# ScalarE places running sums into PSUM before the products: a diffusion step on one core

## The chip, the cores and the metric

The kernel runs on one core of one Trainium2 chip. A core has a matrix engine (TensorE, PE in the profile), which multiplies tiles of 128 by 128 with tiles of 128 by 512 and adds the products up in PSUM (8 banks of 128 by 512 f32), a vector engine (VectorE, DVE), a scalar engine (ScalarE, ACT), GpSimd (POOL) and SyncE (SP), which here issues the DMAs. Each engine runs its own instructions in the order in which the program emits them, and waits on semaphores for what other engines and DMAs deliver. The metric is the time of one execution on the device, in microseconds.

## The reference, cut to what matters

One layer of a diffusion backbone, for 128 context tokens and 128 latent tokens:

```
h   = RMSNorm(x) * (1 + scale1) + shift1          # scale, shift, gate: SiLU(cond) @ w_ada + b_ada
p   = h @ w_in                                    # 2048 x 8704: q, k, v of two mixers, two gates
o_A = window attention(q_A, k_A, v_A);  o_B = neighbourhood attention(q_B, k_B, v_B)
m   = (sigmoid(gate_A) * (o_A @ w_br_a) + sigmoid(gate_B) * (o_B @ w_br_b)) @ w_out
x   = x + gate1 * m
h2  = RMSNorm(x) * (1 + scale2) + shift2
x   = x + gate2 * (relu(h2 @ w_up) ** 2 @ w_down)  # w_up 2048 x 8192, w_down 8192 x 2048
```

Both token groups use the same weights. Everything is f32, and the result must be near f32. The outputs are the new x of both groups and the new keys and values.

## The kernel before

**Products.** TensorE takes its operands rounded (`F32R`). Each f32 operand is therefore split in two, a rounded part (hi) and what the rounding left (lo), and a product is three matmuls: hi x hi, hi x lo, lo x hi. The weights come in 456 steps, `wsteps`. A step is one DMA of 512 KB (a tile of 128 by 1024: two slices of 128 rows, 512 columns), its preparation and, as a rule, 12 matmuls: 2 slices, 2 token groups, 3 products. The preparation (`prep`) is a ScalarE copy `wH<-raw` (hi, line 93) and a VectorE subtraction `wL<-raw,wH` (lo, line 241). For the steps of `LO_DMA` the lo part is made without VectorE: ScalarE writes minus hi (line 247), and a DMA of the GpSimd queue adds the raw weight to it (line 248).

**Order.** The program is written out step by step by `run`. At step i it emits the loads up to i + RUN[i] (each load is registered four steps ahead of its use), then the preparations up to i + LOOK[i], then the matmuls of step i, then whatever was hung on step i: `ex(i, ...)` first, then `at(i, ...)` in the order of registration. The tables (LOOK, RUN, DOTS and so on) are plain lists in the program. A position in the emitted order is a position in the queue of every engine: an instruction that waits holds up all that its engine has behind it.

**SBUF and PSUM.** All big tiles are taken from one pool of 48 buffers of 4 KB per partition (`G`). PSUM has two pools of four banks: `pacc` for running sums, `paux` for the rest. A unit of work is 512 output columns for both token groups and takes two banks of `pacc`, so two units fit at a time.

**First part (steps 0 to 71).** The nine units of q, k and v (`first_units`) go through their 16 slices in five chunks of 2, 2, 2, 4 and 6 slices (`CHUNKS`), because the normalised h appears slice by slice: `mod_pair` multiplies the condition with w_ada (64 small matmuls for each pair of slices, line 308), `make_h` scales (lines 354 and 356) and `split_h` splits (lines 93 and 97). A chunk has all nine units, each with 1, 1, 1, 2 or 3 steps. The last two units of a chunk stay in PSUM and open the next one; the others leave: after the first time ScalarE copies the sums to SBUF (`first_evac`), after later chunks VectorE adds them to the sums there (line 406, two instructions per unit). Chunk 4 is steps 27 to 44, in the order qB0, qB1, kB0, kB1, vB0, vB1, kvA, qA0, qA1; chunk 5 is steps 45 to 71.

**Middle (steps 72 to 215).** Gates, branch products, `w_out`, and the first two of the 16 column blocks of `w_up`. VectorE also forms the adaLN rows that do not come from `mod_pair`: `dot` (line 1339), 1024 elements at a time, hung on the steps of `DOTS1`, `DOTS` and `DOTS2`.

**Last part (steps 216 to 455).** For p = 0 to 7 the step list holds the next pair of blocks of `w_up` (`up_pair`, 16 steps) and then the four units of `w_down` over the pair p (`down_unit(p, n)`, n = 0 to 3, 4 steps each). In `up_pair`, 8 pairs of steps are worked either plainly (24 matmuls) or fast, by seven products in place of eight (21 matmuls, more VectorE and ScalarE work: lines 1184 to 1194); FAST lists the fast positions. The sum over p lies in SBUF, in `dsum[n]`: p = 0 is copied there by ScalarE; later ones are added by VectorE (line 1269, two instructions), or, for the units in `SUM_DMA`, copied by ScalarE to a tile that a DMA of the GpSimd queue adds (line 1273). After p = 6, `gate_sum` multiplies the sum with gate2 and adds it to x (lines 1250 and 1251, four VectorE instructions a unit); the products of p = 7 go through `resid` (lines 916 and 917) to the output. `gate_rows` (line 1352) is a TensorE transposition of the rows that the dots leave, hung on the first `down` step after the last dot.

The functions that the change touches:

Of the kernel before, what the change touches and what calls it, by code (L numbers as in the profile page):

```python
# [46 lines left out]
LOOK = "652422234122454433223333332123333453344534333554455544344534333543324554444555556665556644444333333333332222122312344544555434333333342344333334333323445566643344456656433344434444445455564546555553444554322466554554433333333434334533333333333654544332334455643444555653315536554523333334543233333332223323365455455443222212233432443334434642333334444544534434333333333325434222223333434444444434555642255242433444442233554442233242223342112224442233345544"  # L47
RUN = "300000000000010212223333322222222221111122244455544355434445554334554445555775654544345434444445665543321222222212444444444444442222222232223344444455544544444444555454454466677755566555554543365434343355445756644443566664333312222234552332223333334545332333333333322211133333332233311101234434433332332112444444442454322211333343334323233334544422742222212223445554422333233322222211222333333435767445344121210002232000233455555566567556433435335553333334"
CONST_AT = [67, 70]
XL_DMA = []  # L50
ADA_AT = [None, 4, 13, 16, 21, 36, 32]
XS_AT = {1: 13, 2: 18, 3: 29}
POST = {('kvA', 0): [67, 70, 75], ('qA', 0): [70, 73, 78], ('qA', 1): [72, 74, 80], ('kB', 0): [77, 86, 90], ('qB', 0): [82, 84, 93], ('kB', 1): [87, 92, 95], ('qB', 1): [90, 93, 96]}
JOBS = [[79, 80, 80, 87, 93], [81, 83, 88, 90, 93], [87, 87, 89, 90, 96], [93, 93, 96, 102, 105], [96, 97, 100, 105, 112], [102, 103, 107, 112, 123], [105, 107, 111, 118, 123], [112, 115, 118, 121, 123]]
SS_AT = [41, 57, 73, 75, 135, 139]
T_AT = [4, 4]
PREP_IN = [6, 4]
DOTS = [33, 39, 42, 45, 47, 48, 49, 50, 53, 55, 55, 55, 60, 65, 69, 70, 73, 75, 80, 84, 90, 91, 92, 93, 95, 100, 101, 103, 103, 104, 108, 110, 111, 112, 115, 118, 120, 122, 123, 124, 126, 127, 128, 129, 130, 132, 133, 134, 137, 138, 138, 143, 144, 145, 147, 150, 153, 157, 159, 160, 166, 167, 170, 172, 173, 174, 175, 176, 178, 178, 179, 183]
DOTS2 = [230, 232, 234, 235, 236, 237, 240, 243, 255, 263, 265, 269, 270, 288, 300, 300, 306, 328, 328, 331, 333, 334, 358, 360, 362, 364, 368, 368, 391, 391, 395, 399]
STAT_AT = [-1, 0, 10, 11]  # L60
T_PAIR = [[10, 8], [6, 8], [8, 10], [5, 7], [10, 13], [8, 9], [12, 11]]
P_PAIR = [[5, 2], [2, 4], [3, 5], [-1, 3], [5, 8], [3, 3], [7, 4]]
M_TE = (3,)
M_AT = [1, 3, 8]
FLIP = 1
P_UP = [2, 2]
T_UP = [7, 5]
COL = {"qA": 0, "kvA": 1024, "qB": 1536, "kB": 2560, "vB": 3584, "gA": 4608, "gB": 6656}
# [3 lines left out]
def tile_hybrid_step(ctx: ExitStack, tc: tile.TileContext, a):  # L72
# [209 lines left out]

    def mm3(acc, stat, st, first, last, order=(0, 1)):

        wh, wl = st["hl"]
        for k in range(2):
            kk = 2 * st["half"] + k
            for tb in order:
                sh, sl = stat(kk, tb)
                f, l = first and k == 0, last and k == 1  # L290
                pe.matmul(acc[tb], sh, wh[:, k, :], start=f, stop=False)  # L291
                pe.matmul(acc[tb], sh, wl[:, k, :], start=False, stop=False)  # L292
                pe.matmul(acc[tb], sl, wh[:, k, :], start=False, stop=l)  # L293

# [76 lines left out]

    open_acc = {}

# [4 lines left out]

    def start_steps(u, k0, nk, held, hold):


        box = {}

        def mm(st, kt):
            if kt == 0:
                box["acc"] = open_acc.pop(u) if held else [bank("acc", pacc) for _ in range(2)]
            acc = box["acc"]
            wh, wl = st["hl"]
            last = kt + 2 == nk
            for k in range(2):  # L390
                g, kg = divmod(k0 + kt + k, 4)
                for tb in range(2):
                    sh, sl = hH[g][:, kg, tb, :], hL[g][:, kg, tb, :]
                    pe.matmul(acc[tb], sh, wh[:, k, :], start=kt == 0 and k == 0 and not held, stop=False)  # L394
                    pe.matmul(acc[tb], sh, wl[:, k, :], start=False, stop=False)  # L395
                    pe.matmul(acc[tb], sl, wh[:, k, :], start=False, stop=last and k == 1 and not hold)  # L396
            if not last:
                return
            if hold:
                open_acc[u] = acc  # L400
                return
            if u not in units:
                first_evac(u, acc)
                return
            for tb in range(2):
                dve.tensor_tensor(units[u][:, tb, :], units[u][:, tb, :], acc[tb], op=OP.add)
# [117 lines left out]

    def unit(w, c0, ktiles, stat, evac, key, order="both"):

        box = {}
        n = len(ktiles)
        for j, k0 in enumerate(ktiles):
            def mm(st, j=j):  # L530
                if j == 0 and st["half"] == 0:
                    box["acc"] = [bank("acc", pacc) for _ in range(2)]
                mm3(box["acc"], stat(j), st, j == 0 and st["half"] == 0, j == n - 1 and st["half"] == 1)
                if j == n - 1 and st["half"] == 1:
                    evac(box["acc"])
            add_w(w, k0, c0, mm, key)
# [525 lines left out]

    def last_unit(w, c0, ktiles, stat, evac_s, key):

        box = {"hl": {}}
        n = 2 * len(ktiles)

        def mms(q, tb):
            wh, wl = box["hl"][q]
            for k in range(2):  # L1070
                sh, sl = stat(q // 2)(2 * (q % 2) + k, tb)
                pe.matmul(box["acc"][tb], sh, wh[:, k, :], start=q == 0 and k == 0, stop=False)
                pe.matmul(box["acc"][tb], sh, wl[:, k, :], start=False, stop=False)
                pe.matmul(box["acc"][tb], sl, wh[:, k, :], start=False, stop=q == n - 1 and k == 1)

        for j, k0 in enumerate(ktiles):
            def mm(st, j=j):
                q = 2 * j + st["half"]
                if q == 0:
                    box["acc"] = [bank("acc", pacc) for _ in range(2)]  # L1080
# [176 lines left out]

    def down_unit(p, n):
        def evac(acc):
            by_pool = 4 * p + n in SUM_DMA  # L1260
            if p == 0 or by_pool:
                part = G(f"dsum{n}").rearrange("p (s n) -> p s n", s=2)
            for s in range(2):
                if p == last:
                    out_s(acc, n, s)
                elif p == 0 or by_pool:
                    copy(part[:, s, :], acc[s])
                else:
                    dve.tensor_tensor(dsum[n][:, s, :], dsum[n][:, s, :], acc[s], op=OP.add)
            if p == 0:  # L1270
                dsum[n] = part
            elif by_pool:
                pool.dma_start(dsum[n], part, accum_op=OP.add)

        def stat(j):
            return lambda kk, tb: (aH[PIECES[p][j]][:, kk, tb, :], aL[PIECES[p][j]][:, kk, tb, :])
        if p == last and n == 3:
            last_unit(a["w_down"], 512 * n, [4 * j for j in PIECES[p]], stat, lambda acc, s, *c: out_s(acc, n, s, *c), ("down", p, n))
            return
        unit(a["w_down"], 512 * n, [4 * j for j in PIECES[p]], stat, evac, ("down", p, n))  # L1280
        if p == last - 1:
            at(end_of(("down", p, n)) + 6, lambda: gate_sum(n))
# [227 lines left out]
```

## Time and profile before

| | |
|---|---|
| median of 3 runs | 1329.12 us (1329.07 to 1329.39) |
| the profiled execution: span from first to last instruction | 1327.5 us |
| median less that span | 1.6 us |
| PE busy | 1314.7 us, 99% |
| DVE busy | 1179.5 us, 89% |
| ACT busy | 796.3 us, 60% |
| POOL busy | 49.9 us, 4% |
| mean granted TensorE clock | 0.999 |

The profiled execution's own time is not given apart from its span; the 1.6 us between span and median are taken as what lies around the instructions. In the table of slices each digit is the busy share of a fortieth of the span. A matmul's busy time is its latency, and the next one starts before it ends, so a rate is read from starts. A row of groups gives line, engine, operation, tiles, count, busy time and the mean of one, then the idle time before them. A row of the timeline gives start, duration and, in brackets, how long the engine had been idle and who ended it.

### The profile page before, as it was taken

What the parts mean: (1) busy time and instruction counts of PE and PEld (TensorE: products, weight loads), DVE (VectorE), ACT (ScalarE), POOL (GpSimd) and SP (SyncE); (2) the same over time, 40 slices, a digit from 0 to 9 for tenths busy, and PEclk for the clock granted to TensorE, in tenths of its full rate; (3) what the DMA queues carried; (4) which work ended last, traced back from release to release, by engine and by line L of the source; (5) the groups of instructions that cost most, each with busy time, mean ns of one, the idle gap of its engine ahead of it and who ended that gap; (6) DMA issues with size and microseconds to landing.
All of it is one profiled execution on the core that took longest, in us unless ns stands there. A gap on an engine that the chain in (4) does not pass through costs nothing.

```text
span 1327.5 us, 18042 instructions
## 1 busy us (share of the span) xinstructions
PE 1314.7 (99%) x6414; PEld 1066.7 (80%) x6415; DVE 1179.5 (89%) x1529; ACT 796.3 (60%) x973; POOL 49.9 (4%) x61
## 2 busy tenths in 40 slices
PE   8999999999999999999999999999999999999998
PEld 4777788788888878888888888888888888878886
DVE  4588999988898999999779998998999999989595
ACT  5634443467655546645677766767767567676560
POOL 0000000511000000000000000000000000000000
PEclk9999999999999999999999999999999999999999
DMA  9999997978589999996568956988969597788962
GB/s 372 408 409 409 409 387 278 389 263 272 188 310 351 359 390 331 375 370 239 191 229 262 302 222 229 276 290 276 278 223 298 203 305 248 273 224 283 312 208 100
DMA packets 147546, 389.62 MB, mean 294 GB/s; under 512 B 51712, under 2 KB 52928, under 8 KB 147456
## 3 DMA queue, kind: packets, MB, share of 16 engines
q1 hardware_dynamic: 144160, 377.11, 79.0%
q0 software_dynamic: 3152, 11.27, 4.3%
q8 instruction: 50, 0.82, 0.2%
q14 instruction: 40, 0.33, 0.1%
q10 hardware_dynamic: 144, 0.08, 0.0%
HBM read 365.58 MB, written 8.16 MB: 282 GB/s over the span
## 4 chain that ended last, share of the span: by engine, by line
PE 94%; DMA 4%; DVE 1%; ACT 0%; POOL 0%; issue 0%; SPq 0%; ACTq 0%
PE acc L291 17%; PE acc L293 17%; PE acc L292 17%; PE Q L1129 6%; PE Q L1131 6%; PE Q L1130 6%; PE acc L394 4%; PE acc L395 4%; PE acc L396 4%; DMA araw<-in_w_pair 3%; PE ps_ada L308 2%; DMA raw<-in_w_in 1%; PE Z L1129 1%; PE Z L1131 1%; PE Z L1130 1%; PE ps_S L719 1%
## 5 line engine op out<-in xcount | busy, mean ns | idle before, releaser
L241 DVE TENSOR_TENSOR wL<-raw,wH 128x1024 fp32r<-128x1024 f32 x379 | 449.9, 1224 | 62.4 <-ACT wH L93 58.0
L93 ACT ACTIVATE wH<-raw 128x1024 fp32r<-128x1024 f32 (+1 forms) x395 | 394.5, 1044 | 129.5 <-PE acc L396 21.5
L394 PE MATMUL acc<-wH,hH 128*128 128x512 f32 x276 | 109.1, 395 | 0.0
L396 PE MATMUL acc<-wH,hL 128*128 128x512 f32 x276 | 107.5, 390 | 0.0
L395 PE MATMUL acc<-wL,hH 128*128 128x512 f32 x276 | 107.5, 390 | 0.0
L291 PE MATMUL acc<-wH,hH 128*128 128x512 f32 x256 | 101.3, 396 | 0.0
L293 PE MATMUL acc<-wH,hL 128*128 128x512 f32 x256 | 99.7, 390 | 0.0
L292 PE MATMUL acc<-wL,hH 128*128 128x512 f32 x256 | 99.7, 389 | 0.0
L1339 DVE CUSTOM_DVE_ANT_0 junk<-aT,cB,cols 128x1024 bf16<-128x1024 f32 x56 | 71.7, 1286 | 0.0
L1339 DVE CUSTOM_DVE_ANT_0 aT<-aT,cB,cols 128x1024 f32<-128x1024 f32 x56 | 71.4, 1281 | 0.2
L93 ACT ACTIVATE tH<-t 128x1024 fp32r<-128x1024 f32 x32 | 33.9, 1060 | 51.9 <-DVE t L1184 44.5
L394 PEld LDWEIGHTS acc<-wH,hH 128*128 128x128 f32 x276 | 51.8, 188 | 13.6 <-issue 2.9
L396 PEld LDWEIGHTS acc<-wH,hL 128*128 128x128 f32 x276 | 51.8, 188 | 11.0
L395 PEld LDWEIGHTS acc<-wL,hH 128*128 128x128 f32 x276 | 51.9, 188 | 10.3
L293 PEld LDWEIGHTS acc<-wH,hL 128*128 128x128 f32 x256 | 48.1, 188 | 10.1
L291 PEld LDWEIGHTS acc<-wH,hH 128*128 128x128 f32 x256 | 48.1, 188 | 9.8 <-ACT wH L93 0.4
L292 PEld LDWEIGHTS acc<-wL,hH 128*128 128x128 f32 x256 | 48.1, 188 | 9.4
L93 ACT ACTIVATE uH<-raw 128x1024 fp32r<-128x1024 f32 x32 | 34.0, 1063 | 30.0 <-DVE raw L1189 29.0
L1235 ACT ACTIVATE up<-up 128x1024 f32<-128x1024 f32 x28 | 29.7, 1062 | 28.3 <-DVE up L1229 27.9
L308 PE MATMUL ps_ada<-araw,cpad 128*32 128x256 f32 x640 | 39.3, 382 | 2.6 <-DMA araw<-in_w_pair 2.5
L93 ACT ACTIVATE fTa<-pTa 128x2048 uint16<-128x2048 uint16 x16 | 40.5, 2534 | 2.1 <-PE acc L293 1.5
L1184 DVE TENSOR_TENSOR t<-raw 128x1024 f32<-128x1024 f32 x32 | 39.1, 1221 | 2.9 <-PE Q L1131 1.7
(641 smaller groups left out, 3291.7 us busy)
## 6 DMA issues: line engine op xcount, KB each, us to landing
raw<-in_w_in SPq DMA_DIRECT2D x133, 512.0 KB, 9.5
raw<-in_w_down SPq DMA_DIRECT2D x128, 512.0 KB, 5.7
araw<-in_w_pair SPq DMA_DIRECT2D x80, 512.0 KB, 10.0
aT<-in_w_gT SPq DMA_DIRECT2D x64, 512.0 KB, 6.8
raw<-in_w_up SPq DMA_DIRECT2D x64, 512.0 KB, 5.1
raw<-in_w_upF SPq DMA_DIRECT2D x64, 512.0 KB, 5.3
aT<-in_w_adaT SPq DMA_DIRECT2D x48, 512.0 KB, 9.9
raw<-in_w_out SPq DMA_DIRECT2D x32, 512.0 KB, 10.3
```

The source lines that it names most:

```text
L93: act.activation(out, in_, AF.Copy)
L241: dve.tensor_tensor(st["lo"], st["raw"], st["hi"].bitcast(F32), op=OP.subtract)
L291: pe.matmul(acc[tb], sh, wh[:, k, :], start=f, stop=False)
L292: pe.matmul(acc[tb], sh, wl[:, k, :], start=False, stop=False)
L293: pe.matmul(acc[tb], sl, wh[:, k, :], start=False, stop=l)
L394: pe.matmul(acc[tb], sh, wh[:, k, :], start=kt == 0 and k == 0 and not held, stop=False)
L395: pe.matmul(acc[tb], sh, wl[:, k, :], start=False, stop=False)
L396: pe.matmul(acc[tb], sl, wh[:, k, :], start=False, stop=last and k == 1 and not hold)
L1129: pe.matmul(acc, stat[0], hi, start=f, stop=False)
L1130: pe.matmul(acc, stat[0], lo, start=False, stop=False)
L1131: pe.matmul(acc, stat[1], hi, start=False, stop=l)
L1339: dve.tensor_tensor_reduce(out, box["raw"], cB[s, tag], 1.0, dst if second else baT[:, part, fb:fb + 1], OP.mult, OP.add, dst)
```

## The change

Sums that lay in SBUF are no longer added to by VectorE after the products. ScalarE copies them into the two PSUM banks ahead of the unit (`seed`), the products of the unit add onto them (no matmul of it has the start flag), and ScalarE copies the whole sum out again. In the first part this is done in chunks 4 and 5 (`SEED_IN`, c = 3 and 4) for all units but the two that stay open: 14 units. The seed of a unit is hung on the first step of the unit before it, one step ahead in chunk 4, two in chunk 5. In the last part it is done for n = 1, 2, 3 (`SEED_N`) and p from 1 on: 21 units; the seed is hung three steps before the unit's first, so that two steps lie between. For p = 7 the bank then holds the whole sum, and `gate_sum` is left out for these n. Only n = 0 is still added by VectorE, and no unit of `SUM_DMA` is left that uses the DMA: all its entries are seeded units. The tables are new: 110 of the 456 digits of LOOK and 222 of RUN differ.

```diff
-DOTS1 = [11, 15, 27, 29, 29, 30, 32, 35]
+DOTS1 = [14, 18, 24, 29, 31, 32, 42, 42]
-FAST = {1: (0, 3, 7), 2: (0, 4, 5, 7), 3: (0, 2, 4, 5, 7), 4: (0, 2, 4, 5, 7), 5: (0, 3, 4, 5, 7), 6: (0, 2, 5, 6, 7), 7: (0, 1, 3, 5, 7)}
-SUM_DMA = [5, 6, 11, 13, 16, 19, 21, 23, 25]
+FAST = {1: (0, 1, 3, 7), 2: (0, 2, 5, 7), 3: (0, 2, 4, 5, 7), 4: (0, 2, 3, 5, 7), 5: (0, 1, 3, 4, 7), 6: (0, 2, 4, 5, 7), 7: (0, 1, 3, 5, 7)}
+SUM_DMA = [5, 6, 10, 11, 13, 23, 30]
+SEED_IN = {3: 0, 4: 0}
+SEED_N = (1, 2, 3)
+SEED_AT = 3
-LO_DMA = [89, 107, 131, 176, 184, 233, 292, 314, 319, 404]
+LO_DMA = [88, 115, 131, 165, 176, 184, 196, 233, 314, 319, 404]
...
-DOTS = [33, 39, 42, 45, ...
+DOTS = [31, 39, 46, 47, ...
...
     def first_evac(u, acc):
...
+    def seed(box, src):
+        box["acc"] = [bank("acc", pacc) for _ in range(2)]
+        for tb in range(2):
+            copy(box["acc"][tb], src[:, tb, :])
...
-    def start_steps(u, k0, nk, held, hold):
+    def start_steps(u, k0, nk, held, hold, seed_step=None):
...
-            if kt == 0:
+            if kt == 0 and not seeded:
                 box["acc"] = open_acc.pop(u) if held else [bank("acc", pacc) for _ in range(2)]
...
-                    pe.matmul(acc[tb], sh, wh[:, k, :], start=kt == 0 and k == 0 and not held, stop=False)
+                    pe.matmul(acc[tb], sh, wh[:, k, :], start=kt == 0 and k == 0 and not held and not seeded, stop=False, **kw)
...
+        if seeded:
+            sown.add(u)
+            at(seed_step, lambda: seed(box, units.pop(u)))
...
-            start_steps(u, k0, nk, c > 0 and j < 2, c < ends and j >= nf - 2)
+            seed_step = len(wsteps) - nk // 2 + SEED_IN[c] if c in SEED_IN and j >= 2 else None
+            start_steps(u, k0, nk, c > 0 and j < 2, c < ends and j >= nf - 2, seed_step)
...
-    def unit(w, c0, ktiles, stat, evac, key, order="both"):
+    def unit(w, c0, ktiles, stat, evac, key, seed_from=None):
...
+        if seed_from:
+            at(len(wsteps) - SEED_AT, lambda: seed(box, seed_from()))
...
     def down_unit(p, n):
+        seeded = p > 0 and n in SEED_N
         def evac(acc):
-            by_pool = 4 * p + n in SUM_DMA
+            by_pool = 4 * p + n in SUM_DMA and not seeded
+            whole = p == 0 or by_pool or seeded
...
-                elif p == 0 or by_pool:
+                elif whole:
                     copy(part[:, s, :], acc[s])
...
-        if p == last - 1:
+        if p == last - 1 and n not in SEED_N:
             at(end_of(("down", p, n)) + 6, lambda: gate_sum(n))
```

More of the change, by code (lines that the diff above doesn't have):

```diff
@@ L281, in run, with mm3 @@
                 fn()
-    def mm3(acc, stat, st, first, last, order=(0, 1)):
+    def mm3(acc, stat, st, first, last, seeded=False):
         wh, wl = st["hl"]
@@ L287, in mm3 @@
             kk = 2 * st["half"] + k
-            for tb in order:
+            for tb in range(2):
                 sh, sl = stat(kk, tb)
[L290 to L293, printed above, removed]
+                f, l = first and k == 0 and not seeded, last and k == 1
+                kw = {"skip_group_check": True} if seeded else {}
+                pe.matmul(acc[tb], sh, wh[:, k, :], start=f, stop=False, **kw)
+                pe.matmul(acc[tb], sh, wl[:, k, :], start=False, stop=False, **kw)
+                pe.matmul(acc[tb], sl, wh[:, k, :], start=False, stop=l, **kw)
     def pair_load(box, nsub, fb):
```

70 lines of the change are left out of this document (40 added, 30 removed).

## The prediction

> **What bounds the kernel now.** I read the page's busy shares and slices first, then the chain that ended last, then who TensorE (PE) waited for.
>
> ```profile
> span 1327.5 us, 18042 instructions
> PE 1314.7 (99%) x6414; PEld 1066.7 (80%) x6415; DVE 1179.5 (89%) x1529; ACT 796.3 (60%) x973; POOL 49.9 (4%) x61
> PE   8999999999999999999999999999999999999998
> PE 94%; DMA 4%; DVE 1%; ACT 0%; POOL 0%; issue 0%; SPq 0%; ACTq 0%
> ...
> PE ps_ada L308 <- DMA araw<-in_w_pair: 2.5, 5, 0.6
> PE acc L473 <- ACT hH L93: 1.3, 2, 0.9
> PE ps_gr L1352 <- DVE gc_g L1339: 1.0, 1, 1.0
> ```
>
> PE is busy in every slice and carries 94% of the chain; VectorE (DVE) and ScalarE (ACT) carry almost nothing. All that PE waited for the waits list in a few microseconds. So an instruction taken from VectorE is worth nothing by itself: only fewer matmuls, or fewer and shorter gaps of PE, move the end.
>
> A matmul's price is its start-to-start time. These two starts lie twelve matmuls (one step) apart, so 2.72/12 = 0.227 us each:
>
> ```profile
> 143.79 0.39 PE L396 MATMUL acc<-wH,hL 128*128 128x512 f32 x1
> ...
> 146.51 0.39 PE L396 MATMUL acc<-wH,hL 128*128 128x512 f32 x1
> ```
>
> **Gaps of PE.** After the start-up (steps 0 to 4, whose tables are the same up to step 6) the timeline shows three places where PE pauses:
>
> ```profile
> 146.82 3.23 PE L308 MATMUL ps_ada<-araw,cpad 128*32 128x256 f32 x56
> 150.33 0.64 PE L308 MATMUL ps_ada<-araw,cpad 128*32 128x256 f32 x8 [0.28 <-DMA araw<-in_w_pair]
> ...
> 943.95 0.39 PE L1131 MATMUL Q<-YB,h20L 128*128 128x512 f32 x1
> 944.38 0.50 PE L1129 MATMUL Q<-tH,sH 128*128 128x512 f32 x1
> ...
> 1177.53 0.39 PE L293 MATMUL acc<-wH,a10L 128*128 128x512 f32 x1
> 1178.88 0.28 PE L1352 MATMUL ps_gr<-ident,gc_g 128*32 128x128 f32 x1 [0.96 <-DVE gc_g L1339]
> ```
>
> They are 0.28 us (weights of w_ada late), 0.43 - 0.23 = 0.2 us (line 1129 starts 0.43 after its neighbour), and 0.96 us (the transposition of `gate_rows` waits for the last dot). Together 1.44 us: with the matmuls saved, this is all that a better order behind the start-up can win.
>
> **The change part by part.**
>
> *TensorE.* FAST has 33 positions in place of 32 (p = 1 gains position 1). A plain pair of steps is 24 matmuls, a fast one 21, so three go: 3 x 0.227 = -0.68 us, on the path. A seeded unit has as many matmuls as before.
>
> *VectorE.*
>
> ```profile
> L406 DVE TENSOR_TENSOR u_qA<-u_qA,acc x12: 680/683/689, 61.7 to 195.6; 128x512 f32<-128x512 f32 x12
> L1269 DVE TENSOR_TENSOR dsum<-dsum,acc x30: 678/684/697, 833.1 to 1279.2; 128x512 f32<-128x512 f32 x30
> L1250 DVE TENSOR_TENSOR dsum<-dsum,g x8: 682/684/686, 1262.0 to 1296.7; 128x512 f32<-128x512 f32 x8
> L241 DVE TENSOR_TENSOR wL<-raw,wH 128x1024 fp32r<-128x1024 f32 x379 | 449.9, 1224 | 62.4 <-ACT wH L93 58.0
> L1194 DVE TENSOR_TENSOR uL<-raw,uH 128x1024 fp32r<-128x1024 f32 x32 | 39.0, 1219 | 0.0
> L1189 DVE TENSOR_TENSOR raw<-raw 128x512 f32<-128x512 f32 x32 | 22.1, 692 | 1.1
> ```
>
> The first part loses 14 units x 2 adds = 28 x 0.683 = 19.1 us. The last part has 30 adds at line 1269 (24 units less nine in SUM_DMA, twice) and keeps 12 (n = 0, p = 1 to 6): 18 x 0.684 = 12.3 us. `gate_sum` keeps one unit of four: 12 x 0.69 = 8.2 us. The new fast position costs four full-width operations at 1.22 and three half-width ones at 0.69, less two subtractions: 4.9 + 2.1 - 2.4 = +4.5 us. Sum -35 us of 1179.5, all beside PE: nothing by itself. The +4.5 lies in steps 218 and 219, where VectorE has a hole to put it:
>
> ```profile
> 692.71 1.23 DVE L241 TENSOR_TENSOR wL<-raw,wH 128x1024 fp32r<-128x1024 f32 x1 [5.50 <-ACT wH L93]
> ```
>
> That 5.5 us covers it; without the cover up to 4.5 us would fall on PE.
>
> *ScalarE.*
>
> ```profile
> L93 ACT ACTIVATE dsum<-acc x26: 574/598/604, 741.7 to 1257.4; 128x512 f32<-128x512 f32 x26
> L93 ACT ACTIVATE YB<-raw 128x512 fp32r<-128x512 f32 x32 | 19.9, 622 | 2.6 <-PE Q L1131 1.6 <-DMA raw<-in_w_upF 0.6 <-PE Q L1130 0.3
> L247 ACT ACTIVATE wL<-wH 128x1024 fp32r<-128x1024 f32 x10 | 10.6, 1061 | 1.3 <-ACT wH L93 0.8 <-PE acc L292 0.2
> ```
>
> No row shows a copy from SBUF into PSUM. It is bounded by the copy out of PSUM (0.598) and the copy within SBUF (0.622); I take 0.6. First part: 28 seeds and 28 copies out; last part: 42 seeds and 18 more copies out (36 seeded, less 18 of SUM_DMA). 116 x 0.6 = +70 us. The fast position adds about 1.7. LO_DMA names step 319, which becomes the second half of a fast position: its rounding and its line 247 are done and not used, 2 x 1.06 = +2.1 us. 796.3 becomes about 870 us, 66% of the span: hidden, as long as no seed stands behind a wait (below).
>
> *Queues.* GpSimd loses the nine DMAs of line 1273 and gains one of line 248; nothing new is behind them on POOL. SP issues the same weights; two of the aT loads move behind the w_ada load of step 36 (DOTS1 has two entries at 42), which brings that load forward. Those two dots and `make_h` for the last slices now end at steps 43 and 44 in place of 41 and 42, and are needed at 47: two steps of 2.72 us lie between where four lay. I cost this at nothing, because the adds that stood between on VectorE are gone; without that, up to the 5.4 us of the two lost steps could show.
>
> *The old gaps.* The 0.28 goes with the two loads moved. The 0.2 us at 944.38 is a wait that hangs on the accumulating DMA, which is gone:
>
> ```profile
>   PEld Q L1129: 0.5, 1
> ```
>
> (this row stands under "who waited for it" of dsum). At `gate_rows` LOOK falls by one at steps 399 and 400 and by two at 401, so VectorE reaches the dot one subtraction (1.22) earlier, more than the 0.96 that it was late. All three go: -1.44 us. What ends last there is still that dot, now 0.3 us ahead.
>
> *The new waits.* 35 units now wait for two seeds. In the last part a bank is free one copy-out (2 x 0.6) after unit n - 2 ends, and the next unit begins a unit later, 48 x 0.227 = 10.9 us: the seed's 1.2 fits many times. Chunk 4 has the tight places, since there a unit lasts two steps, 5.4 us, and ScalarE stands in line behind VectorE:
>
> ```profile
> 145.63 0.88 ACT L356 ACTIVATE xnT<-xnT,shT,scT 128x128 f32<-128x128 f32 x2 [4.42 <-DVE scT L336]
> 150.88 0.63 ACT L93 ACTIVATE hH<-xnT 128x512 fp32r<-128x512 f32 x1 [4.37 <-DVE xnT L354]
> ...
> 147.79 1.28 DVE L406 TENSOR_TENSOR u_kB<-u_kB,acc 128x512 f32<-128x512 f32 x2
> 150.90 0.50 PE L394 MATMUL acc<-wH,hH 128*128 128x512 f32 x1
> ```
>
> The seed of vB1 is hung on step 35, behind this `split_h` (hH). As the rows stand it would end at 150.88 + 0.63 + 1.2 = 152.7, and PE needs it at 150.90: 1.8 us late. But VectorE is what holds hH, and by step 35 it has two adds less for each of kB0 and kB1 (2.7 us) and two dots jobs less (9 entries up to step 35 become 7; four dots):
>
> ```profile
> L1339 DVE CUSTOM_DVE_ANT_0 junk<-aT,cB,cols 128x1024 bf16<-128x1024 f32 x56 | 71.7, 1286 | 0.0
> ```
>
> 4 x 1.29 = 5.1 us. hH then comes up to 7.8 us earlier, and 1.8 is covered. Bounds: nothing, or 1.8 for this unit. The seed of qA0 stands behind the `split_h` of step 39:
>
> ```profile
> 160.71 0.63 ACT L93 ACTIVATE hH<-xnT 128x512 fp32r<-128x512 f32 x1
> ...
> 162.45 0.39 PE L394 MATMUL acc<-wH,hH 128*128 128x512 f32 x1
> ```
>
> 160.71 + 0.63 + 1.2 = 162.5, as late as PE's need at 162.45, and vB1's copy out (1.2) now stands before it: bounds nothing, if ScalarE is earlier, and 1.3. I put one new gap in the sum, between these ends, with the size of the largest old one: +0.96.
>
> *Sum.* -0.68 - 1.44 + 0.96 = -1.16 us against a span of 1327.5, so 1326.3; the median lies 1.6 above the span, so 1327.9 us, or 1329.12 - 1.2. About 0.2% (2.66 us) is what a measurement of this kernel can tell from no change, so this counts as none.
>
> **The rivals.**
>
> *Only the matmuls count* (the old gaps stay, or come back elsewhere in full): 1329.1 - 0.7 = 1328.4. For it: none of the gaps is touched in its own line. Against it: each has a removed cause.
>
> *Seeds behind ScalarE's waits: slower.* Place: chunk 4, seeds hung on steps 33 to 41 behind `make_h` and `split_h`. Point: hH later than 149 us. Price: 1.8 for vB1, and as a late unit makes its own copy-out and the seed after next late, the same for kvA and qA0: 5.4 - 0.7 = +4.7, so 1333.8; with two units 1332.0. For it: 4.42 and 4.37 us of ScalarE waiting on VectorE. Against: the 7.8 us.
>
> *Too few banks.* A seed takes its banks a half to a full unit before the products do. Where VectorE still empties them late, PE pauses:
>
> ```profile
> 126.11 0.39 PE L394 MATMUL acc<-wH,hH 128*128 128x512 f32 x1
> ...
> 129.63 1.28 DVE L406 TENSOR_TENSOR u_qB<-u_qB,acc 128x512 f32<-128x512 f32 x2
> ```
>
> qB1 ended at 126.11 and its banks were free at 130.91, and two seeds more make 132.1, 6.0 us; a two-step unit gives 5.4, so 0.6 short, and seven units of chunk 4 would make 4.2: 1329.1 - 0.7 + 4.2 = 1332.6. Against it: w_ada matmuls lie in between here, and only qB0 and qB1 are still emptied by VectorE. [...]
>
> *More than the limit.* Start-up waits shrink too: all 1.44, the 0.68 and half of the 2.5 us of the first row of PE's waits, 3.4 us: 1325.7. Against it: the loads up to step 6 are the same.
>
> **How the numbers follow.** Forecast 0.50, only the matmuls 0.24, seeds late 0.14, banks 0.04, more 0.08. Slower by over 0.2% (above 1331.8): 0.14 + 0.04 = 0.18. Faster by over 0.2% (below 1326.5): 0.08. Within: 0.74. The range runs from just under the forecast with no new gap (1326.9) to just over two late seeds (1332.0): 1326.4 to 1332.2. What is left out is most of the 0.08 below and about half of the 0.18 above.
>
> **What would show it.** Right: 5373 products in place of 5376; no idle time before line 1352; about 70 copies of 0.6 us into acc; VectorE near 1145 us, ScalarE near 870; no row for line 1273. Wrong: PE idle released by ScalarE at the first matmul of a seeded unit (seeds late), gaps of the same size at many units (banks), or PE waiting for wL at steps 218 to 223 (the fast position uncovered) or for hL at step 47.

## The result, and the profile after

The changed kernel takes 1330.76 us (median of 20 runs, 1328.88 to 1333.88), the kernel before 1329.09 us beside it (20 runs, 1328.65 to 1330.46). The ratio is 1.0013 (95% interval 1.0006 to 1.0020): about 1.7 us slower. By the bound of 0.2% this is still no change, but the sign is the opposite of the forecast of 1327.9, and it is outside what the runs leave open. The profiled execution took 1331.95 us with a span of 1330.2 us. Runs of the changed kernel spread over 5 us, so a profile shows one execution out of these; this one lies 1.2 us above the median.

The page of the changed kernel: span, busy times, PE's slices and its share of the chain.

```profile
span 1330.2 us, 18031 instructions
PE 1316.3 (99%) x6411; PEld 1067.2 (80%) x6412; DVE 1150.2 (86%) x1476; ACT 858.3 (65%) x1093; POOL 45.0 (3%) x53
PE   8999999999999999999999999999999999999998
PE 95%; DMA 4%; DVE 1%; issue 0%; ACT 0%; SPq 0%; ACTq 0%; DVEq 0%
```

PE has three instructions fewer (6411 for 6414), VectorE 29 us less, ScalarE 62 us more: the bulk of the change went as costed, and PE is still the bound. Its waits name the difference (engine, line, releaser; total us, times, longest):

```profile
PE ps_h L1022 <- DVE h2f L1014: 2.4, 1, 2.4
PE ps_ada L312 <- DMA araw<-in_w_pair: 2.1, 4, 0.6
PE acc L490 <- ACT hH L96: 1.3, 2, 0.9
PE Q L1152 <- ACT dsum L96: 0.3, 1, 0.3
```

The first row is new. It is the transposition of `h2f` in `norm2_T`, in the second norm; no step of the prediction touches it. (Line numbers have moved: 1002 is now 1022, 241 is 244, 93 is 96, 994 is 1014, 949 to 951 are 969 to 971.) The timeline of PE after, at that place, which is unit out3, the last of `w_out` (steps 192 to 199). Out3 goes through its matmuls in two passes, one per token group; after the first pass `norm2` normalises that group into `h2f`, and among the matmuls of the second pass PE transposes `h2f`:

```profile
636.75 0.39 PE L971 MATMUL acc<-wH,m1L 128*128 128x512 f32 x1
639.49 1.06 PE L1022 MATMUL ps_h<-ident,h2f 128*128 128x128 f32 x8 [2.35 <-DVE h2f L1014]
...
640.96 0.63 PE L971 MATMUL acc<-wH,m2L 128*128 128x512 f32 x1
641.39 0.63 PE L969 MATMUL acc<-wH,m2H 128*128 128x512 f32 x1
...
642.67 1.75 PE L1022 MATMUL ps_h<-ident,h2f 128*128 128x128 f32 x8
644.18 0.48 PE L969 MATMUL acc<-wH,m2H 128*128 128x512 f32 x1
```

Two losses follow each other. PE idles: 639.49 - 636.75 - 0.227 = 2.51 us by starts. Then its matmuls start 0.43 us apart instead of 0.227, and eight transpositions take 1.75 instead of 1.03. The stretch from the first transposition to the matmul behind the second group is 644.18 - 639.49 = 4.69 us; the same 22 instructions took 3.05 before, in the timeline of PE of that kernel:

```profile
638.39 0.39 PE L951 MATMUL acc<-wH,m2L 128*128 128x512 f32 x1
638.62 1.03 PE L1002 MATMUL ps_h<-ident,h2f 128*128 128x128 f32 x8
...
641.67 0.48 PE L949 MATMUL acc<-wH,m3H 128*128 128x512 f32 x1
```

So 1.64 us of slow matmuls stand behind 2.51 us of waiting. The windows of the changed kernel show it as the granted clock (the third figure from the end of each row):

```profile
core 0: us, PE busy (x) PEld busy (x) DVE busy (x) ACT busy (x) POOL busy (x), PEclk, DMA share, GB/s
636.00:638.00 2.00, 1.14 (x6) 0.60 (x4) 2.00 (x3) 2.00 (x4) 0.00 (x0) 1.00 0.25 20
...
640.00:642.00 2.00, 2.00 (x11) 1.67 (x9) 1.33 (x4) 1.76 (x5) 0.00 (x0) 0.68 0.03 8
642.00:644.00 2.00, 2.00 (x10) 1.70 (x9) 0.72 (x2) 0.62 (x2) 0.00 (x0) 0.50 0.31 29
644.00:646.00 2.00, 2.00 (x11) 1.69 (x10) 1.54 (x5) 2.00 (x6) 0.00 (x0) 0.97 0.93 369
```

Windows of 0.1 us at the two ends show 1.00 up to 640.70, 0.58 in the next one and 0.50 from 640.80; then 0.50 up to 644.10, 0.85 in the next one and 1.00 from 644.20. So the granted clock was 0.50 from 640.72 to 644.13, 3.41 us.

Laid side by side by the start of each step, the two profiled executions differ like this (after less before; each row is the change within the stretch):

| steps | us | what |
|---|---|---|
| 36 to 44 | -0.53 | the pause for the w_ada weights is gone |
| 192 to 197 | +0.41 | PE waits once for wL at 626 us |
| 198 and 199 | +4.18 | the stall above |
| 216 to 231 | -0.63 | the new fast position |
| 248 to 263 | +0.64 | first product of the next fast pair waits for ScalarE's copy of `dsum` |
| 296 to 327 | -0.40 | the pause at 944 us is gone |
| 400 to 403 | -1.04 | the wait at `gate_rows` is gone |
| the rest | +0.09 | |
| all | +2.72 | 1330.2 - 1327.5 |

What caused the stall is read from the timeline of VectorE, here in the changed kernel:

```profile
634.69 0.15 DVE L1005 TENSOR_SCALAR ms<-ss 128x1 f32<-128x1 f32 x1
635.45 3.50 DVE L244 TENSOR_TENSOR wL<-raw,wH 128x1024 fp32r<-128x1024 f32 x3 [0.60 <-ACT wH L96]
638.86 0.88 DVE L1014 TENSOR_SCALAR h2f<-x,r 128x512 f32<-128x512 f32 x2
```

And in the kernel before, VectorE at the same place:

```profile
634.48 0.15 DVE L985 TENSOR_SCALAR ms<-ss 128x1 f32<-128x1 f32 x1
635.23 2.36 DVE L241 TENSOR_TENSOR wL<-raw,wH 128x1024 fp32r<-128x1024 f32 x2 [0.60 <-ACT wH L93]
637.51 0.88 DVE L994 TENSOR_SCALAR h2f<-x,r 128x512 f32<-128x512 f32 x2
```

Two entries of the tables met here. `T_AT[0]`, the place of the transpositions in the second pass, went from 4 to 3, which puts them half a step (six matmuls, 1.36 us) earlier in PE's queue. `PREP_IN[0]`, how far `norm2` brings the preparations of weights forward between the statistic (`ms`) and `h2f`, stayed 6, but LOOK fell at step 199 (4 to 3) and around it, so three preparations are still to be emitted there instead of two: 3.50 us instead of 2.36, and from `ms` to `h2f` 4.17 us instead of 3.03, 1.14 more. (Of the digits of RUN 45 differ between the kernels, not 222; 110 of LOOK is right.)

Two smaller terms belong to the sum. When PE waits for `h2f`, its first transposition starts 0.63 us behind the start of `h2f` (639.49 - 638.86). In the kernel before it starts 1.11 behind (638.62 - 637.51), so `h2f` was 0.48 us ahead of PE. And the statistic itself is later in the changed kernel: PE's last matmul starts 2.06 us after `ms` (636.75 - 634.69), against 3.91 - 1.36 = 2.55 before, because VectorE, busy with preparations, starts the work in front of it 0.5 us late. 1.36 + 1.14 + 0.49 - 0.48 = 2.51 us, the idle time by starts.

### The profile page after: what moved, and what is told of

Read it like the earlier page. It is cut to its first block, busy times and chain, and to the rows that moved or that the text cites. A ratio compares the mean times of both kernels' runs of the same rounds, so it can differ in the third digit from the quotient of the medians.

```text
span 1330.2 us, 18031 instructions
## 1 busy us (share of the span) xinstructions
PE 1316.3 (99%) x6411; PEld 1067.2 (80%) x6412; DVE 1150.2 (86%) x1476; ACT 858.3 (65%) x1093; POOL 45.0 (3%) x53
## 4 chain that ended last, share of the span: by engine, by line
PE 95%; DMA 4%; DVE 1%; issue 0%; ACT 0%; SPq 0%; ACTq 0%; DVEq 0%
PE acc L295 17%; PE acc L296 17%; PE acc L297 17%; PE Q L1152 6%; PE Q L1154 6%; PE Q L1153 6%; PE acc L406 5%; PE acc L408 5%; PE acc L407 5%; PE ps_ada L312 2%; DMA araw<-in_w_pair 2%; DMA raw<-in_w_up 1%; PE ps_S L739 1%; PE Z L1152 1%; PE Z L1154 1%; PE Z L1153 1%
## 5 line engine op out<-in xcount | busy, mean ns | idle before, releaser
L1367 DVE CUSTOM_DVE_ANT_0 aT<-aT,cB,gc_g 128x1024 f32<-128x1024 f32 x32 | 40.4, 1278 | 0.1
```

Source lines behind the costliest of these rows:

```text
L1367: dve.tensor_tensor_reduce(out, box["raw"], cB[s, tag], 1.0, dst if second else baT[:, part, fb:fb + 1], OP.mult, OP.add, dst)
```

## The experiments

All times are medians beside the kernel before on the same chip, 11 runs if nothing else is said (8 for the kernel without the first part's seeds, one for the changed kernel profiled again); "before" is 1329.0 to 1329.2 there unless given. Where two changed kernels are compared, they may have run on different chips, and each interval is about 0.0009 to either side. Kernels with useless matmuls send them to a PSUM bank that nobody reads; the rest of the work is whole in all of them.

**The transpositions half a step later.** The changed kernel with

```diff
-T_AT = [3, 4]
+T_AT = [4, 4]
```

> The changed kernel with one table entry back: the transpositions of h2f in the second pass of out3 stand after its fifth step again (T_AT[0] 4, not 3). Theory 'one wait in out3': PE reaches them 6 x 0.227 = 1.36 us later, so of the 2.35 us idle before line 1022 about 1.0 stays; too short an idle to lower the clock after it, so the nine matmuls at 0.427 us are back at 0.227 as well (about 1.7 us). Time 1330.8 - 1.4 - 1.7 = 1327.7. Rival 'seeds': the loss lies in the 35 seeded units and ScalarE's load, the out3 wait is a symptom: no more than 1.4 us comes back, 1329.4 or more.

1328.97 us, ratio 0.9999 (0.9990 to 1.0008): 1.8 below the changed kernel. The idle time is 0.91 us in place of 2.35, no matmul behind it is slow (granted clock 1.00 from 637 to 646 us), and out3 costs 1.85 us more than before in place of 4.59 (0.41 + 4.18). The place is right; one entry alone does not empty it.

**One preparation fewer before `h2f`.** The changed kernel with

```diff
-PREP_IN = [6, 7]
+PREP_IN = [5, 7]
```

> The changed kernel with one table entry moved: PREP_IN[0] 5, not 6, so two preparations and not three stand between the statistic of group 0 and its h2f. Theory 'one wait in out3': h2f comes one VectorE subtraction, 1.14 us, earlier; idle before line 1022 1.2 us, no lowered clock, 1330.8 - 1.1 - 1.7 = 1328.0. Rival 'seeds': 1329.6 or more.

1328.92 us, ratio 0.9999 (0.9991 to 1.0008). The idle time is 0.88 us, again without slow matmuls (granted clock 1.00 there). Each entry alone is worth about 1.8 us: it takes some 1.4 us off the idle time, and the slow matmuls do not come.

**Both.** `T_AT = [4, 4]` and `PREP_IN = [5, 7]`.

> Both entries at once (T_AT[0] 4, PREP_IN[0] 5). Theory 'one wait in out3': no idle before line 1022, full clock throughout out3, and the rest of the change shows: 0.7 for three matmuls and about 1.9 of old gaps less than before, 0.6 of a new one at the first product of Q7 in up2: about 1326.7, faster than before by 2.4 us. Rival 'seeds': 1329 or slower.

1328.45 us, ratio 0.9998 (0.9989 to 1.0007). No idle time is left before the transpositions. That is 2.3 below the changed kernel, but 1.7 above the 1326.7 expected: other small waits remain (in the profile three of 0.3 us each: for wL in out3, for `dsum` and for a seed at step 404). Its timeline of PE also has slow matmuls elsewhere, at the start-up, behind three gaps for w_ada (granted clock 0.60 from 41.5 to 45 us), which cost about 1.5 us:

```profile
43.30 0.63 PE L406 MATMUL acc<-wH,hH 128*128 128x512 f32 x1
43.73 0.63 PE L407 MATMUL acc<-wL,hH 128*128 128x512 f32 x1
```

**The gap filled.** The changed kernel, with ten useless matmuls (10 x 0.227 = 2.27 us) in front of the first group of transpositions:

```diff
-        return {(p, j): [T(0), T(1), S(0)], ...
+        return {(p, j): [lambda: fill(10) if p else None, T(0), T(1), S(0)], ...
```

> The changed kernel, and ten matmuls with no use (128x512, into a bank of their own) in front of the transpositions of group 0, so that PE works while it would wait; outputs are unchanged. Theory 'the idle costs twice, once itself and once by the clock after it': PE reaches the transpositions at the same time (ten x 0.227 = 2.3 against 2.35 idle), but the clock stays full: matmuls after it at 0.227, 1.7 us less than the changed kernel, 1329.1, and a narrower spread of the runs. Rival 'the clock has no part': same time as the changed kernel, 1330.8.

1330.08 us, ratio 1.0008 (0.9999 to 1.0016). The wait is just as long, but PE works through it, and the matmuls behind it run at full speed (granted clock 1.00 from 637 to 646 us): out3 costs 2.27 us over before, exactly the filling. In this kernel's profile the slow part is gone. The median lies between the two expectations, 0.7 us below the changed kernel's, which is within the intervals: what the slow clock costs is shown by the profiles, not by these medians.

**The tables planted in the kernel before.** No seed, no new fast position; only LOOK and RUN of steps 176 to 207, `T_AT[0]` = 3 and step 196 in LO_DMA.

```diff
-T_AT = [4, 4]
+T_AT = [3, 4]
-LO_DMA = [89, 107, 131, 176, 184, 233, 292, 314, 319, 404]
+LO_DMA = [89, 107, 131, 176, 184, 196, 233, 292, 314, 319, 404]
...
```

> The kernel before, with nothing of the change but its tables for out3: LOOK and RUN of steps 176 to 207, T_AT[0] 4 to 3, and step 196 in LO_DMA. No seed, no new fast position. If the stall in out3 comes from the moved tables alone, PE idles about 2.3 us before the first transposition of h2f, runs at about half rate for some 3.4 us behind it, and the time is 2 to 4 us above the kernel before: 1331 to 1333. If the stall needs the seeds or the emptier VectorE of the changed kernel, there is no such gap and the time is that of before, 1329.0.

1330.92 us, ratio 1.0014 (1.0005 to 1.0023), as slow as the changed kernel. The timeline of PE of this kernel, with the gap and without slow matmuls behind it:

```profile
638.61 1.06 PE L1002 MATMUL ps_h<-ident,h2f 128*128 128x128 f32 x8 [1.86 <-DVE h2f L994]
...
640.21 0.40 PE L949 MATMUL acc<-wH,m2H 128*128 128x512 f32 x1
640.45 0.40 PE L950 MATMUL acc<-wL,m2H 128*128 128x512 f32 x1
```

So the moved tables make a stall by themselves, without seeds and without the emptier VectorE: 2.02 us by starts. The other half of the expectation failed, for the granted clock stayed at 1.00 here from 637 to 646 us; why it fell behind 2.35 and 2.08 us of idle time and not behind the 1.86 here is not shown.

**The tables of before put into the changed kernel**, for the same steps, `T_AT[0]` = 4, step 196 out of LO_DMA.

> The changed kernel with the tables of before for out3 (LOOK and RUN of steps 176 to 207, T_AT[0] = 4, step 196 not in LO_DMA); seeds, fast position and all other tables stay. If all that was lost lies in out3, neither the gap before the transpositions nor the one for wL at 626 us is left, and the sum of the prediction without its new gap holds: -0.7 for the matmuls, about -1.4 for the old gaps, +0.3 for the new one at the first product of up2: 1329.0 - 1.8 = 1327.2. If the seeds cost something that no gap shows, or a new gap opens elsewhere, 1328.4 or more.

1329.73 us (1328.22 to 1332.25), ratio 1.0005 (0.9996 to 1.0013), a miss: 2.5 above the expected 1327.2. The profiled execution (1328.22, its fastest) has only 0.28 us idle before the transpositions, and steps 192 to 199 add 0.47 us. What the slower runs lose is not seen in it, but each run's mean granted clock is on record: the three slowest (1330.90, 1332.24 and 1332.25) have 0.998, the five with 1.000 lie at 1328.2 to 1329.8.

One sum gives the idle time by starts in all of these profiles: 1.36 if `T_AT[0]` is 3, 1.14 if three preparations are left, the time by which VectorE starts `t<-g,acc` (the work in front of the statistic) later against PE's matmuls than in the kernel before, less the 0.48 that `h2f` was ahead:

| kernel | sum | measured |
|---|---|---|
| changed | 1.36 + 1.14 + 0.49 - 0.48 = 2.51 | 2.51 |
| changed, profiled again (below) | 1.36 + 1.14 + 0.23 - 0.48 = 2.25 | 2.24 |
| tables planted in the kernel before | 1.36 + 1.14 + 0.00 - 0.48 = 2.02 | 2.02 |
| transpositions half a step later | 1.14 + 0.42 - 0.48 = 1.08 | 1.07 |
| one preparation fewer | 1.36 + 0.17 - 0.48 = 1.05 | 1.04 |
| tables of before in the changed kernel | 0.92 - 0.48 = 0.44 | 0.44 |

Why VectorE is late by 0 to 0.9 us is not shown.

**The gaps of the start-up filled.** Between 38 and 42 us PE waits three times about 0.6 us for w_ada. Two useless matmuls stand before each of these three blocks:

```diff
         for q in range(4):
+            if fb == 3 and q:
+                for _ in range(2):
+                    pe.matmul(spare, hH[0][:, 0, 0, :], ..., start=True, stop=True)
             pair_mm_q(box, j, fb, q)
```

> The kernel of the run beside it (changed kernel, tables of before for out3), with two useless matmuls (0.45 us) before each of the last three blocks of w_ada matmuls at step 4, where PE otherwise idles three times about 0.6 us between 38 and 42 us. If these gaps sometimes lower the clock (one profile shows matmuls at 0.43 us from 42 to 44 us, 1.4 us lost), the upper part of the runs' spread, some 1.3 us above the lower, goes, and the median is 0.3 to 0.6 us below the run without: 1326.8. If the spread has another source, no difference, or +0.1 for the matmuls.

> The kernel before with the same two useless matmuls ahead of the last three blocks of w_ada matmuls at step 4. The runs of the kernel before lie in two heaps, about 1328.9 and 1330.2. If the upper heap is the lowered clock behind the start-up's gaps, it is gone here: all runs at 1328.5 to 1329.1, median 1328.9. If not, both heaps stay.

1330.59 (ratio 1.0011, 1.0002 to 1.0020) and 1331.14 us (1.0018, 1.0009 to 1.0026): both slower. The condition was wrong: a block of the second norm's w_ada near step 75 has the same number, and the six matmuls ran there again. In the kernel before they added 2.1 us there (steps 72 to 79) and nothing at 38 us. These two say nothing on the question; the next two have the matmuls at step 4 alone.

> The changed kernel with the tables of before for out3, PREP_IN[0] = 5 besides, and two useless matmuls before each of the last three blocks of w_ada matmuls at step 4 alone (the earlier kernels of this kind had them a second time near step 75, which cost 2.0 us there). If the rest of the loss is the 0.4 us gap before the transpositions and a lowered clock behind the start-up's gaps in some runs, neither is left: 1327.3, runs within 1327 to 1328.5. If the runs vary for another reason (small gaps that move from run to run), the median stays at 1328.5 to 1329.7 and the spread at 3 us.

> The kernel before with those six useless matmuls at step 4 and nowhere else. If the upper of the two heaps of its runs (1328.9 and 1330.2) is a lowered clock behind the start-up's gaps, it goes: all runs at 1328.5 to 1329.2. If not, 4 in 10 runs stay near 1330.2.

The changed kernel with the tables of before for out3, `PREP_IN[0]` = 5 and the filling: 1328.23 us (1327.32 to 1328.92), ratio 0.9992 (0.9983 to 1.0001). The kernel before with the filling: 1329.18 us (1328.82 to 1331.73), ratio 1.0001 (0.9992 to 1.0009), with three runs at 1329.99 or above, so the upper heap did not go as expected. (The runs of the kernel before lie in two heaps, about 1328.9 and 1330.2.) Two of these three have a mean granted clock of 1.000, so they were not slowed by the clock. In the kernel before beside it, all seven runs at 1330.0 or above have 0.999 and the twelve fastest 1.000, so the clock may well have a part in that heap; this stays open. The profile of the filled kernel (1329.99 us) loses 1.07 us (860.98 - 859.68 - 0.227) elsewhere, at a product that waits for VectorE, in the timeline of PE:

```profile
859.68 0.39 PE L1136 MATMUL Q<-YB,h20L 128*128 128x512 f32 x1
860.98 0.50 PE L1134 MATMUL Q<-tH,sH 128*128 128x512 f32 x1 [0.91 <-DVE dsum L1274]
```

VectorE in the best version, at the place of the stall, has one preparation before `h2f`:

```profile
635.12 1.23 DVE L244 TENSOR_TENSOR wL<-raw,wH 128x1024 fp32r<-128x1024 f32 x1 [0.61 <-ACT wH L96]
636.26 0.88 DVE L1019 TENSOR_SCALAR h2f<-x,r 128x512 f32<-128x512 f32 x2
```

**Without the first part's seeds** (base: both entries back, 1328.45).

```diff
-SEED_IN = {3: 0, 4: 0}
+SEED_IN = {}
```

> The changed kernel with T_AT[0] = 4 and PREP_IN[0] = 5 (1328.45 when run before) and without the seeds of the first part: VectorE adds the 28 sums again (19 us), ScalarE has 56 copies less. If seeds neither cost nor win by themselves, as the prediction had it, PE shows no new gap in chunks 4 and 5 and the time is 1328.45 within 0.8. If these seeds held up PE without a visible gap, it is faster by over 1: 1327. If VectorE's room in chunks 4 and 5 is needed by the new tables, PE waits there for wL or hH and the time is 1330 or more.

1332.98 us (8 runs, 1331.89 to 1335.57), ratio 1.0031 (1.0020 to 1.0041). The list of what PE waited for names VectorE's wL and `S`:

```profile
PE acc L407 <- DVE wL L244: 2.2, 2, 1.4
PE ps_sel L330 <- ACT S L96: 2.1, 2, 1.6
```

The new tables use the 19 us that the seeds take off VectorE; take the seeds away and that room is missing. This shows that tables and seeds belong together, not that the adds were slower under their own tables.

**Without the last part's seeds** (same base).

```diff
-SEED_N = (1, 2, 3)
-SUM_DMA = [5, 6, 10, 11, 13, 23, 30]
+SEED_N = ()
+SUM_DMA = [5, 6, 11, 13, 16, 19, 21, 23, 25]
```

> The changed kernel with T_AT[0] = 4 and PREP_IN[0] = 5 and without the seeds of the last part; SUM_DMA as in the kernel before, so VectorE and the GpSimd queue add the sums again (12.3 us and nine DMAs) and gate_sum has all four units (8.2 us). If those seeds are worth nothing by themselves, 1328.45 within 0.8, with the 0.2 us gap near 944 back. If they are what makes room for the fifth fast position and takes the wait at gate_rows away, 1329.5 or more, with the gap before line 1352 back; if they cost, 1327.5 or less.

1329.89 us (1328.80 to 1331.49), ratio 1.0005 (0.9996 to 1.0013), 1.4 above its base, though the two intervals overlap (0.9989 to 1.0007 for the base), and this profile has the slow matmuls at the start-up. No gap at `gate_rows` comes back, against the expectation: that gain is LOOK's. New waits for VectorE are in the later fast pairs and down units, in the timeline of PE:

```profile
985.10 0.50 PE L295 MATMUL acc<-wH,a6H 128*128 128x512 f32 x1 [0.34 <-DVE up L1252]
...
1048.82 0.50 PE L1153 MATMUL Q<-XL,h21H 128*128 128x512 f32 x1 [0.21 <-DVE XL L1215]
```

**The changed kernel profiled again.**

> The changed kernel as it is, for a second profile. If the stall in out3 is what a typical run has, PE idles about 2.3 us before the transpositions of h2f here too, and the span is 1328.5 to 1330.5. Open is whether matmuls at 0.43 us stand behind it: if the lowered clock always follows an idle time of that length they do, and out3 has 4.0 to 4.6 us over the kernel before; if only in some runs, they may be missing, and out3 has 2.3 to 2.9 us over it.

1331.12 us (before 1329.89 on that chip), span 1329.3. In its timeline of PE the stall is there again, and so are the slow matmuls:

```profile
638.58 1.38 PE L1022 MATMUL ps_h<-ident,h2f 128*128 128x128 f32 x8 [2.08 <-DVE h2f L1014]
...
641.46 0.63 PE L970 MATMUL acc<-wL,m2H 128*128 128x512 f32 x1
641.89 0.63 PE L971 MATMUL acc<-wH,m2L 128*128 128x512 f32 x1
```

Steps 192 to 199 cost 3.88 us over before, against 4.59 in the first profile. It shows one seed late as well. ScalarE waits 2.33 us for a DMA with two copies of `fTa` behind it, and the seed of the unit at step 404 comes after both; PE waits 0.27 us for it. ScalarE of this execution:

```profile
1178.32 2.53 ACT L96 ACTIVATE fTa<-pTa 128x2048 uint16<-128x2048 uint16 x1 [2.33 <-DMA pTa<-pla]
...
1185.50 1.10 ACT L96 ACTIVATE acc<-dsum 128x512 f32<-128x512 f32 x2
```

And PE, at the unit's first product:

```profile
1186.14 0.50 PE L295 MATMUL acc<-wH,a10H 128*128 128x512 f32 x1 [0.27 <-ACT acc L96]
```

**Is the best version's gain out3 or the filling?** The best version without the filling, alone, then both side by side, and the changed kernel with nothing but the filling:

> The changed kernel with the tables of before for out3 and PREP_IN[0] = 5, without the useless matmuls at step 4 (with them 1328.23, runs within 1.6 us). If those matmuls kept a lowered clock of the start-up away, the median without them is 0.3 to 0.8 higher, with runs up to 1329.5 and above. If they did nothing, 1328.2 and the same narrow spread, and all of the gain is the order of the work in out3.

> The best version (tables of before for out3, PREP_IN[0] = 5, useless matmuls at step 4), beside the same without the matmuls, on one chip. If the matmuls at step 4 keep a lowered clock away, 1328.2 with a spread of 1.6 us, and 0.7 to 1.5 below the version without; if the difference between the two earlier runs was the chip's, both have the same median within 0.4.

> The same without the useless matmuls at step 4. If the lowered clock behind the start-up's gaps falls on some of its runs, 1328.9 to 1329.7 with a spread of over 2.5 us; if not, 1328.2 like the one beside it.

> The changed kernel with nothing but the useless matmuls at step 4. If they are worth 0.7 to 1.5 us wherever they stand, 1329.3 to 1330.1 (1330.76 without); the stall in out3 stays as it is. If they are worth nothing, 1330.8.

Alone, without the filling: 1329.74 us (before 1329.89 on that chip), ratio 1.0002 (0.9993 to 1.0011). Side by side: 1328.40 us with (1327.64 to 1329.45; ratio 0.9993, 0.9985 to 1.0002), 1328.86 us without (1328.29 to 1333.05; 1.0001, 0.9993 to 1.0010). The changed kernel with the filling: 1329.30 us (1328.60 to 1332.78; 1.0008, 0.9999 to 1.0017), seven of its runs at 1328.6 to 1330.0 and four at 1331.3 to 1332.8; two of these four have a mean granted clock of 1.000, so the clock is not the whole of the spread. The spread is narrower with the filling in the best version, as expected of it; but 0.46 us between the medians lies between the two expectations, and the profiles without slow matmuls at the start-up are the rule anyway (two of thirteen executions without the filling have them, none of six with). Whether the filling is worth anything stays open. The profile of the last kernel has the stall in out3 without the slow clock and a span of 1327.2:

```profile
638.34 1.06 PE L1027 MATMUL ps_h<-ident,h2f 128*128 128x128 f32 x8 [1.85 <-DVE h2f L1019]
...
640.18 0.40 PE L975 MATMUL acc<-wL,m2H 128*128 128x512 f32 x1
640.41 0.40 PE L976 MATMUL acc<-wH,m2L 128*128 128x512 f32 x1
```

The best version is 0.7 to 0.9 us below the kernel before in both comparisons, and each interval just reaches 1: a gain of that size is likely, not shown.

## Why the prediction was wrong

*The step that failed: the one new gap, +0.96 at the seed of qA0.* The sum allowed +0.96 for all waits that the change might put in, placed it at the seed of qA0 in chunk 4, and priced the tables only where they touch seeds, dots, w_ada and `gate_rows`. The moves of `T_AT`, LOOK and LO_DMA in out3 have no term at all. There was nothing at qA0; in out3 the profile lost 4.59 us (0.41 for wL, 2.51 idle, 1.64 slow clock, to rounding), in the second profile 3.88. The rows to see most of it were there before: the statistic, two preparations (2.36 us), `h2f`, and `h2f` only 0.48 us ahead of PE. A chain with so little slack, moved 1.36 us earlier at one end and 1.14 us later at the other, must open by 2.0; the planted tables gave 2.02. The sum had no term either for slow matmuls behind an idle time, the 1.64.

*Three matmuls fewer, -0.68:* right. 6411 PE instructions for 6414, and -0.63 us in steps 216 to 231. The 5.5 us hole of VectorE did cover the fast position's +4.5.

*The three old gaps, -1.44:* all three went, and were worth more than their idle time: -0.53, -0.40 and -1.04 us over their stretches, -1.97 in all. Behind w_ada and at the place of the wait at 944 us PE of the changed kernel goes straight on:

```profile
147.67 2.77 PE L312 MATMUL ps_ada<-araw,cpad 128*32 128x256 f32 x48
150.38 0.50 PE L406 MATMUL acc<-wH,hH 128*128 128x512 f32 x1
...
946.44 0.39 PE L297 MATMUL acc<-wH,a5L 128*128 128x512 f32 x1
946.67 0.39 PE L1152 MATMUL Q<-XH,h20H 128*128 128x512 f32 x1
```

*Seeds at nothing:* right for chunks 4 and 5, where no profile lists a wait of PE for a seed, and nearly so for the last part. The assumed 0.6 us per copy measured 0.58 to 0.60 (rows of the tiles' views of the changed kernel; the three figures are the least, median and greatest ns):

```profile
L96 ACT ACTIVATE acc<-dsum x42: 575/581/603, 827.4 to 1305.0; 128x512 f32<-128x512 f32 x42
L96 ACT ACTIVATE acc<-u_kB x8: 594/600/604, 120.9 to 219.4; 128x512 f32<-128x512 f32 x8
```

"The seed's 1.2 fits many times" looked at PSUM alone. The seed also has a place in ScalarE's queue, and at step 404 that queue waits for a DMA; PE waits 0.2 to 0.6 us there in eight of the fourteen profiles with seeds in the last part. In the profile of the changed kernel a copy out, not a seed, was late: +0.64 us at the first product of the pair after it (timeline of PE, changed kernel):

```profile
779.20 0.39 PE L1154 MATMUL Q<-YB,h20L 128*128 128x512 f32 x1
779.93 0.50 PE L1152 MATMUL Q<-tH,sH 128*128 128x512 f32 x1 [0.34 <-ACT dsum L96]
```

*VectorE -35, ScalarE +74 us, both hidden:* -29 and +62, hidden. That VectorE's time is "worth nothing by itself" holds only with tables that do not spend it: without either group of seeds, PE waits for VectorE (the runs without seeds).

*The rivals.* Seeds late in chunk 4 and too few banks did not occur. "Slower" had 0.18 for mechanisms at seeded units; the slower result came from table entries at a place without seeds. That the median of 1330.76 lies inside the range is luck: the range's upper end was set by late seeds, which had next to no part in it.

Taken together: what the change saves is real (-0.63 - 1.97 = -2.60 us in the profile). The idle time in out3 with the two smaller waits (2.51 + 0.41 + 0.64 = 3.56) takes it back and 1.0 us more; the slow clock adds 1.6 when it comes. The 20 runs fit this. A stretch of 3.41 us at half clock takes 0.0013 off the mean, so the nine runs with a mean granted clock of 1.000 had none: their median is 1330.10, 1.0 above the kernel before. The six with 0.998 or less have 1331.98.

## What to carry to other kernels

When tables are made anew, price each entry that moved, also those far from the edit: for each, compare the moved instruction's new place with the end of the work it needs, and look for chains that had no slack. A pause of the bound engine is not worth its length alone when a lowered clock can follow it: here 2.35 us of idle time in out3 were followed by 3.41 us at a granted clock of 0.50, which cost 1.64 us more, while behind 1.86 us the clock stayed at 1.00. Filling such a pause, or keeping it short, saved the second part here even where the wait stayed: out3 cost 2.27 us over before with the pause filled, in place of 4.59. And an engine's freed time is a gain only until the new order has spent it.

## What the runs showed of the hardware

At a granted clock of 0.50 the matmuls start 0.43 us apart in place of 0.227. The windows from 41.5 to 45 and from 637 to 646 us show a clock of 1.00 in thirteen of seventeen profiles. The other four have a stretch at 0.50 in one of them: both profiles of the changed kernel in out3 (mean 0.81 from 637 to 646 us), and the kernels with both entries and without the last part's seeds behind the start-up's three gaps for w_ada (0.60 and 0.61 from 41.5 to 45 us). In the two kernels with useless matmuls at step 4 and near step 75, the matmuls behind step 4 start 0.23 us apart. Where windows hold both ends of a stretch, it lasts 3.4 us, if a mean between 0.50 and 1.00 is taken as a part at each of the two:

| profile | clock falls to 0.50 | back at 1.00 | us |
|---|---|---|---|
| changed | 640.72 | 644.13 | 3.41 |
| changed, profiled again | 639.16 | 642.60 | 3.44 |
| both entries | 40.88 | 44.28 | 3.40 |

In out3 the idle time before the transpositions and the clock around it are:

| profile | idle, us | mean clock, 637 to 646 us |
|---|---|---|
| changed | 2.35 | 0.81 |
| changed, profiled again | 2.08 | 0.81 |
| tables planted in the kernel before | 1.86 | 1.00 |
| changed, with the filling at step 4 | 1.85 | 1.00 |
| transpositions half a step later | 0.91 | 1.00 |
| one preparation fewer | 0.88 | 1.00 |
| tables of before in the changed kernel | 0.28 | 1.00 |

At the start-up the three gaps for w_ada, in order of time, and the clock behind them are:

| profile | gaps, us | mean clock, 41.5 to 45 us |
|---|---|---|
| before | 0.54, 0.64, 0.62 | 1.00 |
| changed | 0.52, 0.64, 0.63 | 1.00 |
| changed, profiled again | 0.58, 0.64, 0.62 | 1.00 |
| both entries | 0.59, 0.64, 0.63 | 0.60 |

So the length of one gap does not decide it: the clock fell behind three gaps of at most 0.64 us in one execution, stayed at 1.00 behind three of nearly the same length in others, and stayed there behind 1.86 us in one piece. What decides it is not shown.
